# The delta-rule heads' q, k and v by seven products in the gated heads' stage, kept in DRAM, and their chains pipelined by pairs

## The chip, the cores and the metric

The kernel runs on one core of a Trainium2 chip. The metric is the device time of one execution in microseconds; the kernel before was timed in three runs. Five engines work side by side: PE (matmul, with PEld for its weight loads), DVE (vector), ACT (scalar), POOL and SP, which issues most of the DMA transfers. `order` blocks below show how instructions stand in an engine's queue, without any time; rows are line, operation, output<-inputs, and size.

## The reference

One layer of a streaming encoder on x of 1024 frames by 1024 columns, and a final norm. `h` is the normed x, and one projection of `h` gives the columns of everything in the first part:

```
q, k, v = silu(conv4(h @ [gq, gk, gv]))     # 8 delta-rule heads of 128 columns, 4 causal taps per column
S_t = a_t (I - b_t k_t k_t^T) S_{t-1} + b_t k_t v_t^T ;  o_t = S_t^T q_t      # in chunks
y_a = (rmsnorm(o) * silu(z)) @ w_branch_gdn
y_b = gated linear attention, 4 heads of 128/256 columns, @ w_branch_gla
x  += (sigmoid(gate_a) * y_a + sigmoid(gate_b) * y_b) @ w_out     # two gates of 1024 columns: 16 blocks of 128
x  += cross-attention over 256 memory rows, 4 heads
x  += relu(h @ w1)^2 @ w2
```

A delta-rule head needs per chunk the inverse of a unit lower triangular matrix made of k's products, and then a scan over the chunks that carries the state S.

## The kernel before

All data are fp32. A dense matmul splits both operands into a high and a low part and runs as three matmuls into one PSUM bank (`mm3`, lines 545, 547, 549; the splits are lines 585 on ACT and 586 on DVE or POOL). The tiles are 128 columns by 512 frames ("a half").

Two ways of projecting are in use. **Directly**, a block of 128 columns is 2 halves x 8 slices of the inner dimension x 3 = 48 matmuls of 128x512 (`g_fm`). **By seven products** (Strassen's scheme on 2x2 blocks: two column blocks, two halves; `wino_w`, `gla_dense`, `joined`), a pair of column blocks, 256 columns, is 7 products x 4 x 3 = 84, and the seven results are combined by ACT copies and DVE additions. The combinations of `h` for it lie ready in tiles `t2`, `t4`, `t6`.

The stages run one behind the other:

- `phase0`: the norm of the memory rows; K and V of the cross-attention (`K0` to `V3`, 128x256 matmuls); sums of squares, norm and splits of x; then, in the order that `ORDER` lists, the folds `Q0` to `Q3` (wq times K) and `O0` to `O3` (V times wo), kept in DRAM (`Gd`, `Ud`), and the merge gates 0 to 2. Gate 3 and the combinations of `h` follow.
- `phase_gla`: the 4 gated heads, all products by sevens; behind each head's own columns one pair of gates (`push_gate_pair`, gates 5 to 12).
- `phase_gdn`: the 8 delta-rule heads in 4 pairs. The columns k, q, v, z of each head are projected directly here (`push_conv`, `push_gdn_z`; 32 blocks); the taps read PSUM half by half (lines 1215 on ACT, 1218 on DVE, and 1221 for the columns at the seam). Per pair: decays (`gdn_decay`: `dm` loaded from the DRAM row `gcd`, its last columns copied to `gl`, lines 1233 to 1244), `gdn_keys` (transposes, norms, `kdt` at 1262, gram matrices and `NT` at 1281), `gdn_subst` (62 dependent small steps, lines 1323 and 1325), `gdn_queries`, `gdn_v`, `gdn_inverse` (1349, 1358), `gdn_scan` (8 chunks; per chunk and head the matmuls 1388, 1389, 1398, 1405, 1415 with DVE steps 1391, 1410, 1419 and ACT steps 1393, 1400 between them), and then norm, output and seven sums of the pair's result.
- `phase_merge`, `phase_out`, `phase_attn`, `phase_mlp`, which the change leaves alone.

The chains hardly fill PE, so dense products wait in a queue (`push`), and between a chain's steps `fill(n)` runs n of their matmuls; `until(name)` runs them up to the end of one product, `drain` runs all. The numbers n stand in tables (`GF`, `NFILL`, `FA` to `FI`). The kernel isn't emitted in this order, though: class `Plan` records the operations, and a list scheduler places each engine's instructions by modelled costs and by priorities that come from their matmuls' places. So an engine's final order is a result. Within an engine it is then fixed: what stands behind a waiting instruction waits too. SP's transfers are in this order as well; 32 transfers of the folds are issued by ACT.

Of the kernel before, what the change touches and what calls it, by code (L numbers as in the profile page):

```python
# [32 lines left out]
DK = 15  # L33
LA, FLU = 3, 84
# [3 lines left out]
DXB = 4  # L38
EXB, THB, GLOV, TE = 6, 1, (0, 2, 4, 6), 1
FA, FB, FC, FD, FE, FG, FH, FI = 18, 24, 30, 20, 48, 24, 3, 0  # L40
SE = ((0, 0, 0, 0, 0, 0, 0, 0), (0, 1, 0, 1, 1, 1, 0, 1), (0, 1, 0, 1, 0, 1, 0, 0))
FF = ((24, 24), (24, 24))
ORDER = ('Q0', 'Q1', 'g0', 'Q2', 'O0', 'g1', 'Q3', 'O1', 'g2', 'O2', 'O3')
XO = (('K3','V1','V3'),('V1','V3','Q1'))
# [14 lines left out]


# [4 lines left out]
GATES = (0, 1, 2, 3)  # L65
OUT = "out_0_dram"
ROUNDS, TOP, PAD, WINDOW, LOAD, HORIZON, LAND, RATE = 4, 228656, 128, 3413, 1283, 30000, 2600, 300
# [9 lines left out]
class Op:  # L77


    dma = port = False  # L80
    table = 0
# [81 lines left out]
class Plan:  # L163
    def __init__(self, tc):
        self.tc, self.marks, self.calls = tc, [], []
        self.ops, self.pools, self.tiles, self.top = [], {}, {}, {"left": [], "right": [], "psum": []}
# [118 lines left out]
    def latest(self, deps, at, end):  # L285
# [8 lines left out]
        while todo:  # L294
            i = todo.pop()
            o = ops[i]
            s = last[i] = at[i] if o.eng == "tensor" else last[i] - o.cost
# [9 lines left out]
    def forward(self, deps, prio):  # L307
# [60 lines left out]

        def take(e, now):

            q, f = now_q[e], now_q["flex"]
            if e in ("vector", "gpsimd") and f and (not q or f[0] < q[0]):
# [37 lines left out]
    def make(self):  # L410
# [4 lines left out]
        for i, ins in enumerate(self.trace()):  # L415
            while marks and marks[0].at <= i:
                self.ops.append(marks.popleft())
            if ins.engine in ENGINES and ins.opcode in OPCODES:
                self.ops.append(Op(ins, i in calls))
        self.ops += marks  # L420
# [58 lines left out]
class Layer:  # L479
# [26 lines left out]

    def psd(self):
        return self.made_in(self.ps, [P, HALF], F32, "d", self.name("pd"), 4)
# [6 lines left out]


# [54 lines left out]
    def rsqrt(self, pool, v, n):  # L571
        nc = self.nc
        y = self.til(pool, [P, 8], "rs_y", bufs=2)[:, :n]
        t = self.til(pool, [P, 8], "rs_t", bufs=2)[:, :n]
        o = self.til(pool, [P, 8], "rs_o", bufs=3)[:, :n]
# [23 lines left out]
    def wpart(self, src, shape, lo_eng=None, lp=None, before=None):  # L599

        raw = self.til(self.wp, [P] + shape, "raw", bufs=RAWS)
        hi = self.til(self.wp, [P] + shape, "wop", F32R, bufs=RING)
        lo = self.til(lp, [P] + shape, "wlo", F32R, bufs=2) if lp else \
# [84 lines left out]
    def phase0(self, xp):  # L688
        nc, a = self.nc, self.a
        with ExitStack() as ctx:  # L690
# [27 lines left out]
            def project(which, u):  # L718
                if u == 0:
                    kv[which] = self.til(sp, [P, 2, NB, MEM], "kv", F32R, bufs=2)  # L720
                dst = kv[which]
                before = [lambda i, j=j: mem_piece(2 * j + i) for j in range(2)] if len(kv) == 1 and u == 0 else [None] * 2
                w = [self.wpart(a[which][u][:, 4 * i:4 * i + 4], [4, 256], nc.vector, sp, before[i]) for i in range(2)]
# [8 lines left out]
                for j in range(2):  # L732
                    o, pt = u * 2 + j, pts[j]
                    nc.scalar.activation(dst[:, 0, o, :], pt[:, :MEM], AF.Copy)
                    nc.vector.tensor_tensor(dst[:, 1, o, :], pt[:, :MEM], dst[:, 0, o, :].bitcast(F32), SUB)

            def fold_q(h):
                kT = kv["wk"]
                w = [self.wpart(a["wqT"][h][:, :, i * HALF:(i + 1) * HALF], [2, HALF], nc.vector, sp) for i in range(2)]
                for fb in range(0, NB, 2):  # L740
                    pt = self.psd()
                    for j in range(2):
                        fs = slice((fb + j) % 4 * P, ((fb + j) % 4 + 1) * P)
                        hi, lo = w[fb // 4]
                        yield from self.mm3(pt[:, j * MEM:(j + 1) * MEM],
                                            [((hi[:, k, fs], lo[:, k, fs]),
                                              (kT[:, 0, 2 * h + k, :], kT[:, 1, 2 * h + k, :])) for k in range(2)])
                    st = self.til(sp, [P, 2, MEM], "gst", bufs=3)
                    for j in range(2):
# [1624 lines left out]
```

## Time and profile before

| | us |
|---|---|
| median of 3 runs | 2144.36 |
| lowest, highest | 2143.95, 2146.76 |
| the profiled execution, its own time | 2143.86 |
| its span in the trace | 2142.1 |
| mean granted clock of TensorE | 0.997 |
| phase 0 with gate 3, from the trace | 0 to about 158 |
| gated heads | about 158 to 553 |
| delta-rule heads | about 553 to 1092 |
| merge, output, attention, MLP | about 1092 to 2142 |

In the rows of the profile an instruction's time is its own, though matmuls overlap their neighbours, so that a row's mean times its count is more than the time that PE spends on it. In the timeline a bracket gives the engine's idle time before the row, and what released it. In the table by stretches each engine has its busy time and its count of instructions.

### The profile page before, as it was taken

To read this page: it belongs to the slowest core of one execution; us is meant where nothing else is said; L and a number is where in the kernel's file an instruction comes from. 1 tells how busy PE (TensorE), PEld (TensorE's weight loads), DVE (VectorE), ACT (ScalarE), POOL (GpSimd) and SP (SyncE) were. 2 spreads that over 40 slices of the span, in tenths; PEclk is the share of its full clock that TensorE was granted. 3 is DMA by queue.
4 is the path that set the end of the run, shared out by engine and by line. 5 is a ranking of instruction groups with operands and counts; after the bars stand their busy time and mean duration, and the time that the engine had idled before them with its cause. 6 is when DMAs were issued, how large, how long until landed. Compare 5 with 4: busy or idle time off the path is not lost.

```text
span 2142.1 us, 30977 instructions
## 1 busy us (share of the span) xinstructions
PE 2119.7 (99%) x11040; PEld 1803.8 (84%) x11040; DVE 1565.9 (73%) x2961; ACT 1173.6 (55%) x2337; POOL 169.7 (8%) x209
## 2 busy tenths in 40 slices
PE   8999999999999999999999999999999999999998
PEld 8888988988888888888888888888888888888887
DVE  7846886667685867959668899469967667567855
ACT  7445665365555646556456455565755557444433
POOL 1000000000121321313110000000000000000000
PEclk9999999999999999999999999999999999999999
DMA  7762122211311211112067662325444446778752
GB/s 257 235 230 75 61 95 81 74 65 70 123 40 50 71 44 50 59 45 74 31 221 255 229 205 89 107 81 187 131 164 148 147 149 215 225 250 288 252 176 99
DMA packets 143580, 291.75 MB, mean 136 GB/s; under 512 B 15161, under 2 KB 23737, under 8 KB 143425
## 3 DMA queue, kind: packets, MB, share of 16 engines
q1 hardware_dynamic: 134576, 281.35, 39.3%
q10 hardware_dynamic: 8848, 8.42, 1.1%
q8 instruction: 86, 1.41, 0.3%
q14 instruction: 70, 0.57, 0.1%
HBM read 208.42 MB, written 81.30 MB: 135 GB/s over the span
## 4 chain that ended last, share of the span: by engine, by line
PE 95%; DVE 2%; DMA 1%; ACT 1%; issue 0%; SPq 0%; POOL 0%; DVEq 0%; ACTq 0%
PE pd L549 22%; PE pd L545 22%; PE pd L547 22%; PE ps L547 6%; PE ps L545 6%; PE ps L549 6%; PE ps L617 2%; PE ps L1358 1%; PE ps L1278 1%; PE ps L1292 1%; PE ps L1398 1%; PE ps L1349 1%; PE ps L1415 1%; PE ps L1093 1%; PE ps L1405 1%; PE ps L1091 1%
## 5 line engine op out<-in xcount | busy, mean ns | idle before, releaser
L585 ACT ACTIVATE wop<-raw 128x512 fp32r<-128x512 f32 (+1 forms) x480 | 319.7, 671 | 402.3 <-PE pd L549 170.8
L586 DVE TENSOR_TENSOR wop<-raw,wop 128x512 fp32r<-128x512 f32 (+1 forms) x441 | 312.8, 712 | 200.7 <-ACT wop L585 195.7
L1218 DVE SCALAR_TENSOR_TENSOR acc<-pd,convw,acc 128x511 f32<-128x511 f32 x144 | 106.5, 742 | 18.3 <-ACT acc L1215 18.1
L549 PE MATMUL pd<-t,wop 128*128 128x512 f32 x236 | 94.1, 399 | 0.0
L547 PE MATMUL pd<-A1b,wop 128*128 128x512 f32 x240 | 93.6, 391 | 0.4 <-DVE A1b L586 0.4
L545 PE MATMUL pd<-A1b,wop 128*128 128x512 f32 x240 | 93.6, 391 | 0.3 <-ACT A1b L585 0.3
L547 PE MATMUL pd<-t,wop 128*128 128x512 f32 x236 | 91.9, 389 | 0.0
L545 PE MATMUL pd<-t,wop 128*128 128x512 f32 x236 | 91.7, 389 | 0.0
L549 PE MATMUL pd<-A1b,wop 128*128 128x512 f32 x228 | 88.7, 390 | 0.0
L585 ACT ACTIVATE whi<-raw 128x512 fp32r<-128x512 f32 x70 | 41.4, 625 | 55.8 <-PE pd L547 34.8
L547 PE MATMUL pd<-A1a,wop 128*128 128x512 f32 x176 | 68.6, 390 | 0.3 <-DVE A1a L586 0.3
L545 PE MATMUL pd<-A1a,wop 128*128 128x512 f32 x176 | 68.5, 389 | 0.0
L549 PE MATMUL pd<-A1a,wop 128*128 128x512 f32 x164 | 65.3, 398 | 0.0
L586 DVE TENSOR_TENSOR wlo<-raw,wop 128x1024 fp32r<-128x1024 f32 (+1 forms) x37 | 43.9, 1192 | 27.7 <-PE pd L549 13.2
L549 PE MATMUL pd<-A0b,wlo 128*128 128x512 f32 x152 | 60.9, 401 | 0.0
L549 PE MATMUL pd<-A1a,wlo 128*128 128x512 f32 x152 | 60.7, 399 | 0.0
L549 PE MATMUL pd<-A0a,wlo 128*128 128x512 f32 x152 | 60.4, 398 | 0.0
L549 PE MATMUL pd<-A1b,wlo 128*128 128x512 f32 x152 | 59.7, 393 | 0.0
L545 PE MATMUL pd<-A0a,whi 128*128 128x512 f32 x140 | 55.8, 399 | 1.0 <-ACT whi L585 1.0
L545 PE MATMUL pd<-A0b,whi 128*128 128x512 f32 x140 | 55.9, 399 | 0.0
L547 PE MATMUL pd<-A0a,whi 128*128 128x512 f32 x140 | 55.9, 399 | 0.0
L545 PE MATMUL pd<-A1a,whi 128*128 128x512 f32 x140 | 55.8, 399 | 0.0
(650 smaller groups left out, 6675.9 us busy)
## 6 DMA issues: line engine op xcount, KB each, us to landing
raw<-in_w_dram SPq DMA_DIRECT2D x120, 256.0 KB, 3.6
raw<-in_w_gdn_dram SPq DMA_DIRECT2D x64, 256.0 KB, 2.7
raw<-in_w_dram SPq DMA_DIRECT2D x32, 512.0 KB, 3.6
e<-ad SPq DMA_DIRECT2D x63, 256.0 KB, 4.5
ad<-q SPq DMA_DIRECT2D x45, 256.0 KB, 2.7
rawa<-ad SPq DMA_DIRECT2D x42, 256.0 KB, 3.7
A0b<-tgd SPq DMA_DIRECT2D x32, 256.0 KB, 5.0
ad<-acc SPq DMA_DIRECT2D x30, 256.0 KB, 2.4
```

Of the source, the lines that this page charges most:

```text
L545: nc.tensor.matmul(out, lh, rh, start=first and i == 0, stop=False, skip_group_check=True)
L547: nc.tensor.matmul(out, lh, rl, start=False, stop=False, skip_group_check=True)
L549: nc.tensor.matmul(out, ll, rh, start=False, stop=last and i == n - 1, skip_group_check=True)
L585: nc.scalar.activation(hi, raw, AF.Copy)
L586: (lo_eng or nc.gpsimd).tensor_tensor(lo, raw, hi.bitcast(F32), SUB)
L617: self.nc.tensor.transpose(pt[:, i * P:(i + 1) * P], s, self.ident)
L1091: nc.tensor.matmul(pk[:, :256], kdt[:, c, :], v[:, c, :], start=True, stop=True)
L1093: nc.tensor.matmul(po[:, :256], AT[:, c, :], v[:, c, :], start=True, stop=(c == 0))
L1218: nc.vector.scalar_tensor_tensor(x, pt[:, 0:HALF - d], tap, x, MUL, ADD)
L1278: nc.tensor.matmul(pt[:, i * P:(i + 1) * P], kc, kc, start=True, stop=True)
L1292: nc.tensor.matmul(pt[:, i * P:(i + 1) * P], k[:, 4 * g + i, :], q[:, 4 * g + i, :], start=True, stop=True)
L1349: nc.tensor.matmul(pt[:, i * 96:(i + 1) * 96], NT[:, u + i, :], PF[:, v + i, 0:96], start=True, stop=True)
```

## The change

**Projections.** The blocks q, k, v of the 8 heads, 12 pairs, and the z of heads 0 and 1 are made by seven products in the gated heads' stage (`push_extra` in place of `push_gate_pair`; `EXTRA` gives the order), and go to DRAM (`gd`). The taps run on whole 1024-wide tiles in SBUF (`taps`, one ACT copy and three DVE steps of 1023, 1022 and 1021 columns); v is turned to frames by transposes there. Gates 5 to 12 and the blocks z2 to z7 are made directly in the delta-rule stage. Over the whole program the matmuls of 128x512 in split fp32 go from 7488 to 7380; those of 128x256 (1248) and the unsplit ones keep their counts.

**Folds.** K and V, unsplit, go to DRAM (`keep`, `kvd`), and the folds run in the delta-rule stage (`fold`). `phase0` gets another order (`EV`): x's loads stand behind those of wk, and the first three gates run half by half.

**Chains.** In the delta-rule stage k, q, v, z are loaded. The substitution of pair p+1 is placed beside the scan of pair p, keys and gram matrices of p+1 ahead of the inverse of p; small operations of a pair's two heads are joined (16 wide). All chunk ends and decays come at once (`gdn_cols`): one DMA reads 64 single elements of `gcd` for each of 128 partitions. `PF` also holds the pair's output. `FILL`, `TFILL`, `PFILL`, `SFILL` say which products fill where.

**Around it.** Pools are laid out by `LAYP`, `LAYW`, `LAYQ`; the pool of `h`'s combinations is cut in three; buffers `EXB` 6 to 5, `DXB` 4 to 6; the planner runs 1 round in place of 4, `RATE` 300 to 390, can ask for matmuls earlier (`sooner`) and keep DVE back for a more urgent step (`held`). In the last gated head, a few products are placed between norm and output (`FJ`).

The core of the diff:

```diff
-    def push_gate_pair(self, sp, u, after=None):
+    def push_qv(self, sp, which, u, after=None):
...
+        def done(i, half, o, src):
+            if o is not src:
+                nc.scalar.activation(o, src, AF.Copy)
+            left[i] -= 1
+            if not left[i]:
+                y[i] = self.dxt(sp)
+                self.taps(y[i], x[i], "qkv".index(which) * GH + 2 * u + i)
+                for g in range(2):
+                    s = slice(g * HALF, (g + 1) * HALF)
+                    nc.scalar.activation(y[i][:, s], y[i][:, s], AF.Silu)
+                    if which != "v":
+                        nc.sync.dma_start(self.gd[which, u][i, :, s], y[i][:, s])
...
+        self.push(f"g{which}{u}", self.gla_dense([self.joined(dest, done)], after))
+        return turn()
...
+EXTRA = (('k', 'v', 't', 'q'), ('v', 't', 'k', 'q'), ('v', 't', 'k', 'q'), ('v', 't', 'k', 'q', 'z0'))
...
+    def taps(self, y, x, blk):
+        cw = self.convw[:, blk]
+        self.nc.scalar.activation(y, x, AF.Copy, scale=cw[:, 3:4])
+        for d in range(1, 4):
+            self.nc.vector.scalar_tensor_tensor(y[:, d:], x[:, :T - d], cw[:, 3 - d:4 - d], y[:, d:], MUL, ADD)
...
+    def gdn_cols(self, sq):
+
+        nc = self.nc
+        g = self.til(sq, [P, GH, NB], "gge", bufs=1)
+        k = self.til(sq, [P, GH, NB], "kf", bufs=1)
+        self.gge, self.kf = (t.rearrange("p h c -> p c h") for t in (g, k))
+        nc.sync.dma_start(g, self.gcd.rearrange("h (c t) -> t h c", t=P)[P - 1:P].broadcast_to([P, GH, NB]))
+        nc.vector.tensor_tensor(self.kf, self.gge, self.tm[:, :, 0], SUB)
+        nc.scalar.activation(k, k, AF.Exp)
+        nc.scalar.activation(g, g, AF.Exp)
...
+            self.gdn_cols(sq)
+            N = GH // 2
+            others(FILL[0])
+            decay(0)
+            run(near(0), PFILL[0])
+            run(self.gdn_gram(sp, heads(0)), PFILL[1])
+            PF = self.gdn_subst(sp, sq, sts[0])
+            for p in range(N):
+                others(FILL[p + 1])
...
+                if p + 1 < N:
+                    run(near(p + 1), TFILL[1])
+                run(self.gdn_queries(sq, heads(p)), TFILL[0])
+                if p + 1 < N:
+                    decay(p + 1)
+                    run(self.gdn_gram(sp, heads(p + 1)), TFILL[2])
+                run(self.sooner(self.gdn_inverse(sts[p], PF), SOON), TFILL[3])
+                if p:
+                    for h, _ in heads(p - 1):
+                        self.until(f"z{h}")
+                    run(self.gdn_out(sp, sq, p - 1, heads(p - 1)), TFILL[4])
+                if p + 1 < N:
+                    PF = self.gdn_subst(sp, sq, sts[p + 1])
+                for e, (h, st) in enumerate(heads(p)):
+                    self.gdn_v(sq, p, e, st)
...
+                for i, _ in enumerate(self.gdn_scan(sq, heads(p))):
+                    if i % 4 == 3:
+                        next(side, None)
+                    self.fill(SFILL)
...
+SFILL, PFILL, TFILL = 4, (4, 12), (4, 14, 4, 10, 12, 10)
+FILL = ((5, 6, 7, 8), ('Q0', 10, 'Q1', 'z6', 'Q2'), (9, 'O1', 'z3', 'Q3'), ('z2', 'z4', 'O0', 'z5', 11, 'O3', 'z7'), ('O2', 12, 13))
...
+EV = (('K2', 1, 'x0'), ('K3', 1, 'kk'), ('V0', 4, 'x1'), ('V1', 0, 's0'), ('V1', 8, 'n0'), ('V2', 8, 's1'), ('V3', 1, 'kv'), ('V3', 4, 'n1'))
```

The first place is the start of the delta-rule stage. SP's queue before the change, where the decays of the first two heads are loaded among weights and stores:

```order
L514 DMA raw_5375<-in_w_gdn_dram 128x512
L514 DMA raw_5379<-in_w_gdn_dram 128x512
L1622 DMA obd_69<-ex_5135 128x512
L1233 DMA dm_5189<-gcd 128x1024
L1233 DMA dm_5203<-gcd 128x1024
L514 DMA raw_5713<-in_w_gdn_dram 128x512
```

SP's queue there in the changed kernel; `gdz` is z0's place in DRAM, `gge` the new load of the chunk ends, and `raw` a gate's weights:

```order
L1016 DMA gdz_106<-dx_6020 128x512
L537 DMA k_824_6131<-gdk_103 128x1024
L537 DMA k_825_6133<-gdk_103 128x1024
L1303 DMA gge_6111<-gcd 128x64x1
L1312 DMA dm_6117<-gcd 128x1024
L1312 DMA dm_6124<-gcd 128x1024
L537 DMA k_914_6474<-gdk_107 128x1024
L537 DMA k_915_6476<-gdk_107 128x1024
L537 DMA q_6470<-gdq_104 128x1024
L537 DMA q_6472<-gdq_104 128x1024
L537 DMA raw_6566<-in_w_gate_dram 128x512
```

And DVE's queue of the changed kernel at the same place:

```order
L1304 TENSOR_TENSOR kf_6112<-gge_6111,tm_196 128x8x8
L1315 TENSOR_TENSOR dm_6117<-dm_6117,tm_196 128x1024
L1315 TENSOR_TENSOR dm_6124<-dm_6124,tm_196 128x1024
L1338 TENSOR_SCALAR vv_6220<-ssk_6135 128x16
L610 TENSOR_TENSOR rs_t_6226<-rs_y_6225 128x16
L1334 TENSOR_TENSOR kdt_827_6136<-ps_6137,kf_6112 128x512
L1334 TENSOR_TENSOR kdt_827_6136<-ps_6165,kf_6112 128x512
L1334 TENSOR_TENSOR kdt_843_6183<-ps_6184,kf_6112 128x512
L611 TENSOR_TENSOR rs_t_6226<-rs_t_6226,vv_6220 128x16
L1334 TENSOR_TENSOR kdt_843_6183<-ps_6202,kf_6112 128x512
L612 TENSOR_SCALAR rs_t_6226<-rs_t_6226 128x16
L619 TENSOR_TENSOR wlo_6565<-raw_6570,whi_6564 128x512
```

The chunk ends, which came out of `dm`, now come by a transfer of their own, ahead of `dm` on SP and at the head of this piece of DVE's queue.

The second place is the scan, on DVE. Before, in the middle of pair 0's scan, the taps of the next head's columns stand between its steps:

```order
L1410 SCALAR_TENSOR_TENSOR S_6489<-S_6417,gge_5198,ps_6487 128x128
L1410 SCALAR_TENSOR_TENSOR S_6493<-S_6421,gge_5212,ps_6491 128x128
L1419 TENSOR_TENSOR v_6086<-ps_6495,qs_6442 128x128
L1419 TENSOR_TENSOR v_6133<-ps_6500,qs_6449 128x128
L1218 SCALAR_TENSOR_TENSOR acc_6352<-pd_6359,convw_176,acc_6352 128x511
L1221 SCALAR_TENSOR_TENSOR acc_6352<-last_6353,convw_176,acc_6352 128x1
L1218 SCALAR_TENSOR_TENSOR acc_6352<-pd_6359,convw_176,acc_6352 128x510
L1391 SCALAR_TENSOR_TENSOR zh_6512<-ps_6509,gneg_180,v_6086 128x128
L1391 SCALAR_TENSOR_TENSOR zh_6519<-ps_6516,gneg_180,v_6133 128x128
```

In the changed kernel, in pair 0's scan, the steps of pair 1's substitution (`pr`, `Pm`, lines 1414 and 1416) stand there:

```order
L1504 TENSOR_TENSOR v_1031_7032<-ps_7346,qs_7300 128x128
L1504 TENSOR_TENSOR v_1032_7035<-ps_7351,qs_7307 128x128
L1414 TENSOR_TENSOR pr_6976<-X_6920,Pm_6922 128x252
L1495 SCALAR_TENSOR_TENSOR S_7340<-S_7271,gge_6111,ps_7338 128x128
L1416 TENSOR_TENSOR Pm_6922<-Pm_6922,pr_6976 128x14x18
L1495 SCALAR_TENSOR_TENSOR S_7344<-S_7275,gge_6111,ps_7342 128x128
L1414 TENSOR_TENSOR pr_6979<-X_6920,Pm_6922 128x247
L1476 SCALAR_TENSOR_TENSOR zh_7376<-ps_7373,gneg_198,v_1031_7032 128x128
L1416 TENSOR_TENSOR Pm_6922<-Pm_6922,pr_6979 128x13x19
L619 TENSOR_TENSOR wlo_7969<-raw_7974,whi_7968 128x512
L1476 SCALAR_TENSOR_TENSOR zh_7383<-ps_7380,gneg_198,v_1032_7035 128x128
```

The taps are gone from the scan, and a substitution step stands ahead of most of its operations.

598 lines of the change are left out of this document (306 added, 292 removed).

## The prediction

> **What bounds the kernel now.** I read the engines' busy time first, then the chain of waits, then the stages.
>
> ```profile
> PE 2119.7 (99%) x11040; PEld 1803.8 (84%) x11040; DVE 1565.9 (73%) x2961; ACT 1173.6 (55%) x2337; POOL 169.7 (8%) x209
> PE 95%; DVE 2%; DMA 1%; ACT 1%; issue 0%; SPq 0%; POOL 0%; DVEq 0%; ACTq 0%
> ```
>
> TensorE is busy for 99% of the span and is 95% of the chain that ended last. So the time is the number of matmuls times what one costs in a full stream, plus the few holes. What one costs is not its row's mean (390 ns): neighbours overlap. I take it from stretches in which PE did nothing but 128x512 matmuls; the table by stretches gives length, then busy time and count of PE, PEld, DVE, ACT, POOL, the granted clock, the DMA share and GB/s.
>
> ```profile
> 0.00:158.00 158.00, 146.85 (x900) 131.90 (x901) 112.30 (x187) 85.32 (x135) 10.51 (x13) 0.98 0.73 243
> 26.20:30.00 3.80, 3.80 (x20) 3.62 (x20) 2.32 (x6) 1.68 (x3) 1.93 (x1) 0.57 1.05 387
> 158.00:553.00 395.00, 394.53 (x2257) 340.80 (x2255) 278.28 (x439) 222.69 (x366) 17.83 (x21) 1.00 0.22 75
> 553.00:1092.00 539.00, 537.99 (x3216) 468.94 (x3216) 400.65 (x1016) 307.62 (x836) 114.17 (x155) 1.00 0.17 59
> 607.00:647.00 40.00, 40.00 (x207) 34.02 (x206) 38.60 (x90) 20.18 (x56) 8.90 (x16) 1.00 0.09 29
> 1700.00:1750.00 50.00, 50.00 (x222) 41.39 (x222) 32.53 (x50) 28.29 (x47) 0.00 (x0) 1.00 0.43 148
> ```
>
> In 1700 to 1750 us, 222 matmuls fill 50.00 us: **225.2 ns each**. The first 158 us are phase 0, 158 to 553 the gated heads, 553 to 1092 the delta-rule heads. PE has 11 us of holes in the first, and 0.5 and 1.0 us in the other two. In 607 to 647 us VectorE is busy for 38.6 of 40 us (pair 0's substitution) and PE still lost nothing, because dense matmuls were there to run.
>
> **The change part by part.**
>
> *Matmuls.* A pair of heads' columns costs 96 matmuls of 128x512 directly and 84 by seven products. Twelve pairs of q, k, v and one of z go from direct to seven products, four pairs of gates go back: (13 - 4) x 12 = 108 fewer, which the two programs' orders show exactly (7488 to 7380 of this shape; 128x256 and the fp32 shapes keep their counts). On a full PE that is 108 x 0.2252 = **-24.3 us**. All else is whether PE stays full.
>
> *Phase 0.* The folds, 192 matmuls of 128x256 and 96 of 128x512 (some 43 us at 0.225 us and half of it), leave for the delta-rule stage; their time is moved, not saved. What stays is the part with the holes:
>
> ```profile
> 5.50 0.79 PE L545 MATMUL pd<-mT,wop 128*128 128x256 f32 x2 [5.50 <-ACT mT L699]
> ...
> 25.31 1.05 PE L628 MATMUL ps<-ones,acc 128*128 128x1 f32 x8 [1.07 <-DVE acc L654]
> ...
> 40.99 1.02 PE L628 MATMUL ps<-ones,acc 128*128 128x1 f32 x8 [0.47 <-DVE acc L654]
> ```
>
> Two holes wait for x's sums of squares (L654). After the first of them the clock was 0.57 over 3.8 us, some 1.6 us more. The change loads x behind all of wk, and places the sums later among the products: these 3 to 5 us may go. Against that, x arrives later, its norm and splits keep their work on DVE and POOL, and the first gate's products now stand where the folds, which don't need x, gave cover. What is late next is x's split, at the first gate. I take 0; bounds -5 and +11, which is two holes like the one of 5.50 us at the start.
>
> *Gated heads' stage.* It grows by 13 pairs and loses 4. VectorE gains the products' combinations (128x512 tensor-tensor, counted 1281 to 1368) and the taps, now 72 of double width in place of 144 and their 72 end columns:
>
> ```profile
> L1218 DVE SCALAR_TENSOR_TENSOR acc<-pd,convw,acc 128x511 f32<-128x511 f32 x144 | 106.5, 742 | 18.3 <-ACT acc L1215 18.1
> L586 DVE TENSOR_TENSOR wlo<-raw,wop 128x1024 fp32r<-128x1024 f32 (+1 forms) x37 | 43.9, 1192 | 27.7 <-PE pd L549 13.2
> ```
>
> A tap on 128x1023 isn't in this trace: not under 0.742, the half-width one, nor over twice that, 1.48; I take 1.3 beside the 1.19 of the 128x1024 row, 94 us where 106.5 stood. Counting the stage's DVE rows in the new order by such durations gives an estimate of 413 us in a stage of some 545, 76%, against 278 in 395, 70%, before. Stretches at 96% (607 to 647) cost PE nothing, so 0. The 146 more SP transfers here and later (901 to 1048 in all) lie beside a DMA share of 0.22: 0.
>
> *Start of the delta-rule stage.* New is one strided load, `gge` from `gcd`: 128 partitions x 64 single elements of 4 bytes, 8192 pieces, 512 for each of 16 engines. Before, the ends came by a DVE copy out of `dm`. The load stands on SP behind the last store of z0 and the loads of k; on DVE `kf` waits for it, and behind `kf` are queued both `dm` subtractions, the `kdt` products that free four PSUM banks, and a gate's weight split. PE has 69 dense matmuls and 16 transposes between z0's last product and the first gram matmul that needs such a bank.
>
> ```profile
> 1092.73 1.09 PE L617 MATMUL ps<-ident,v 128*128 128x128 f32 x8 [0.40 <-DVE v L1443]
> ```
>
> Eight transposes take 1.09 us, so the cover is 69 x 0.2252 + 16 x 0.136 = 17.7 us. What the load itself takes must be bounded from packets of other sizes, and what follows it from the rows of before:
>
> ```profile
> q1 hardware_dynamic: 134576, 281.35, 39.3%
> ...
> oad<-sz SPq DMA_DIRECT2D x12, 256.0 KB, 2.1
> ```
>
> ```profile
> q10 hardware_dynamic: 144, 0.03, 0.4%
> ```
>
> ```profile
> 561.43 0.96 SPq L1233 DMA_DIRECT2D dm<-gcd  x2
> ```
>
> ```profile
> L1242 DVE TENSOR_TENSOR kf<-gl,tm x2: 160/166/172, 569.2 to 571.8; 128x8 f32<-128x8 f32 x2
> L1244 ACT ACTIVATE gge<-gl x2: 191/192/193, 573.2 to 573.3; 128x8 f32<-128x8 f32 x2
> ```
>
> ```profile
> L1238 DVE TENSOR_TENSOR dm<-dm,tm x8: 1217/1226/1227, 572.6 to 959.1; 128x1024 f32<-128x1024 f32 x8
> ```
>
> ```profile
> L1262 DVE TENSOR_TENSOR kdt<-ps,kf x16: 681/691/694, 580.3 to 992.2; 128x512 f32<-128x512 f32 x16
> ```
>
> No 4-byte piece is in the trace. In the first 60 us queue q10 moved 144 packets of some 200 bytes for 0.4% of 16 engines: 0.004 x 960 / 144 = 27 ns each. Packets of 2 KB on q1 over the whole span: 0.393 x 16 x 2142 / 134576 = 100 ns. So 512 pieces are 14 us by the small packets, 51 by the large ones; the lower bound is nothing seen at all, since the pieces might move as fast as their bytes. I take 14, the packets nearest in size. The load leaves some 3 us behind z0's end (the last eviction and store, and SP's issues at 0.48 each), lands at 19 with 2 us of latency (no whole transfer took less than 2.1), and then `kf` (0.2), its exponent (0.2), two `dm` (2.4) and the first `kdt` (0.7) end near 22.5: PE waits **+5 us**, bounds 0 and 42 (3 + 51 + 2 + 3.5 - 17.7). The clock stayed at 1.00 behind the 1 us holes at 553 and 1518 us; I add nothing for it.
>
> The Trainium skill, page "DMA: Bandwidth & Descriptors", section "Rules for kernel authors", says that a strided last dimension becomes one descriptor per element and should be rearranged to be contiguous; the table of its bandwidth section puts a 64-packet transfer at about 10.5 ns per packet. By that, an estimate, 8192 pieces are 86 us and the sum would be some 72 us higher; the row of q10, 27 ns on one of 16 engines (1.7 ns per packet over all 16), speaks against so much.
>
> *Delta-rule stage.* Four rounds; dense work there is 206 us (at 225 ns and half of it) where 357 were, so the chains have less beside them, some 73 us of PE per pair. And pair p+1's substitution now shares VectorE, in order, with pair p's scan.
>
> ```profile
> 1062.22 0.60 DVE L1410 SCALAR_TENSOR_TENSOR S<-S,gge,ps 128x128 f32<-128x128 f32 x2 [1.28 <-PE ps L1405]
> 1062.77 0.52 DVE L1419 TENSOR_TENSOR v<-ps,qs 128x128 f32<-128x128 f32 x2
> 1063.37 0.80 DVE L1391 SCALAR_TENSOR_TENSOR zh<-ps,gneg,v 128x128 f32<-128x128 f32 x2
> 1065.44 0.60 DVE L1410 SCALAR_TENSOR_TENSOR S<-S,gge,ps 128x128 f32<-128x128 f32 x2 [1.27 <-PE ps L1405]
> ```
>
> ```profile
> L1325 DVE TENSOR_TENSOR Pm<-Pm,pr x90: 191/332/427, 609.0 to 1032.4; 128x31 f32<-128x31 f32 x8, 128x135 f32<-128x135 f32 x8, 128x156 f32<-128x156 f32 x8, 128x240 f32<-128x240 f32 x8
> ```
>
> ```profile
> 802.98 0.74 PE L1405 MATMUL ps<-dl,kdt 128*128 128x128 f32 x4 [0.38 <-ACT dl L1400]
> ```
>
> A chunk's cycle can't be under 3.2 us (1062.22 to 1065.44), of which DVE works 1.9. In the new order PE has about 5 us of work per chunk, and DVE puts 7 or 8 substitution steps of 0.33 us into it, 1.9 + 2.6 + splits, some 5 us at most. The slack of 1.8 us per chunk takes a step of at most 0.43 ahead of each of the chunk's three hops on DVE (1.3 us). So PE should mostly stay full: bounds 0 and, with 0.43 lost twice in each of 32 chunks, 27 us. Before, taps of 0.74 us stood in the same place and PE lost 0.38 us at one of them. I take **+3**.
>
> *Rest.* Merge, output, attention and MLP keep their instructions; 0.
>
> Sum: the profiled execution took 2143.9 us (2142.1 span and 1.8 around it; 0.5 below the median of 2144.4): 2143.9 - 24.3 + 5 + 3 = 2127.6, so **2127 us**.
>
> **Rivals.**
> - *All of it hidden.* The strided load is done within the 17.7 us and the scans' steps never meet: 2143.9 - 24.3 = 2119.6, down to 2115 where x's holes go as well. For it: 539 us with 1.0 us of holes under the same kind of order. Against: dense cover shrinks by 151 us. Chance 0.22.
> - *The strided load decides (slower).* At the price of q1's packets, 100 ns, it holds back the first `kdt` until 3 + 51 + 2 + 3.5 = 59.5 us behind z0, and PE waits 42: 2143.9 - 24.3 + 42 + 3 = 2165. It turns the gain into a loss from (24.3 - 3 + 17.7 - 3 - 2 - 3.5) / 512 = 60 ns per piece. For it: a piece can cost a whole access, whatever its size. Against: the 27 ns of q10. Chance 0.12. The Trainium skill's rule on that page is of this kind; by its figure the time would be 2199.
> - *The coupled chains become the bound.* If every hop finds a substitution step ahead of it and the dense matmuls are used up, a pair loses 6 us, 2143.9 - 24.3 + 5 + 24 = 2149. For it: in-order VectorE, one `PF` for substitution, inverse and output. Against: the slack above. Chance 0.18, spread over 2132 to 2152.
> - The forecast, 2121 to 2138 with phase 0's bounds: 0.45. Other holes: 0.03.
>
> **How the numbers follow.** About 0.2%, 4.3 us, is what a measurement of this kernel can tell. Faster: 0.45 + 0.22 + 0.11 of the third rival = 0.78; same 0.07; slower 0.10 of the second and 0.05 of the third and the rest = 0.15. The range leaves out most of the second rival and the tail of the third: 2114 to 2150.
>
> **What would show it.** Right: PE still at 99%, some 108 fewer matmuls, `kf` waiting for a DMA at the stage's start and PE once for `kdt` there by about 5 us; scans 5 us per chunk. The load's landing time tells the second rival, PE idle behind DVE or ACT in scan lines the third, a hole before the first gate's products the head's bound. Wrong would be a gain with PE clearly less busy, or holes in the gated stage, where I priced 76% of VectorE at nothing.

## The result, and the profile after

| | us | ratio to before |
|---|---|---|
| before, median of 22 runs | 2145.06 (2142.95 to 2149.58) | |
| changed, median of 22 runs | 2141.95 (2137.12 to 2145.60) | 0.9983, 95% interval 0.9976 to 0.9989 |
| changed, the profiled execution | 2139.06, span 2137.4, clock 0.998 | |

The kernel is faster by some 3 us (3.1 by the medians, 3.6 by the ratio), where 18 were forecast; the two profiled executions differ by 4.8 us. The page of the changed kernel, busy time and chain:

```profile
PE 2099.2 (98%) x10932; PEld 1781.1 (83%) x10932; DVE 1598.8 (75%) x2851; ACT 1212.3 (57%) x2396; POOL 133.8 (6%) x158
PE 75%; DVE 12%; DMA 7%; issue 2%; ACT 2%; SPq 1%; POOL 1%; DVEq 0%; ACTq 0%; POOLq 0%
```

PE lost exactly the 108 matmuls (11040 to 10932) and 20.5 us of busy time, but its idle time, the span less the busy time, went from 22.4 to 38.2 us, and its part of the chain from 95% to 75%. By stages: what lies behind the delta-rule heads in the kernel before, and then the four stages of the changed kernel (phase 0, gated heads, delta-rule heads, the rest without the tail). The columns are those of the table by stretches: PE's busy time and count come first, the granted clock, the DMA share and GB/s last.

```profile
1095.00:2130.00 1035.00, 1033.82 (x4635) 857.17 (x4635) 763.39 (x1296) 554.56 (x994) 25.20 (x19) 1.00 0.55 181
```

```profile
0.00:97.00 97.00, 90.77 (x589) 83.95 (x589) 81.02 (x131) 58.34 (x103) 3.75 (x9) 1.00 0.67 245
97.00:675.00 578.00, 576.81 (x3093) 491.98 (x3092) 446.33 (x637) 342.08 (x549) 24.47 (x27) 1.00 0.26 86
675.00:1095.00 420.00, 406.74 (x2676) 360.58 (x2675) 310.64 (x782) 262.89 (x753) 82.89 (x103) 1.00 0.51 165
1095.00:2110.00 1015.00, 1005.29 (x4469) 828.10 (x4469) 741.11 (x1249) 539.89 (x971) 18.15 (x13) 1.00 0.56 180
```

Holes in phase 0 shrank from 11.2 to 6.2 us, and its clock, 0.98 over 158 us before, is 1.00, worth another 3 us. In the gated stage they went from 0.5 to 1.2, in the delta-rule stage from 1.0 to 13.3, and behind it, where no line of the kernel changed, from 1.2 to 9.7.

Six of the larger holes, from the timeline of PE in the changed kernel; the bracket has the idle time before the row and what ended it:

```profile
684.90 1.06 PE L650 MATMUL ps<-ident,k 128*128 128x128 f32 x8 [1.60 <-DMA k<-gdk]
701.07 5.47 PE L1358 MATMUL ps<-k 128*128 128x128 f32 x32 [4.67 <-DVE kdt L1334]
...
762.90 3.81 PE L1438 MATMUL ps<-PF,NT 128*128 128x96 f32 x32 [1.10 <-ACT PF L1426]
...
948.36 0.49 PE L1473 MATMUL ps<-S,k 128*128 128x128 f32 x2 [0.68 <-DVE S L1493]
...
1106.66 0.50 PE L580 MATMUL pd<-B1a,wop 128*128 128x512 f32 x1 [0.83 <-DVE B1a L619]
...
1979.58 0.47 PE L578 MATMUL pd<-B0b,wop 128*128 128x512 f32 x1 [2.07 <-DVE A0b L1797]
```

Only one, the second, is the wait that the prediction had named and sized. Behind the heads one place can be found in both programs: the start of the merge's first product (`pd<-B0a`), with 4589 matmuls from there to the end in each. First the kernel before, then the changed one:

```profile
1110.00:2142.10 1032.10, 1022.70 (x4589) 847.73 (x4587) 764.13 (x1306) 551.96 (x992) 25.88 (x20) 1.00 0.55 180
```

```profile
1092.75:2137.40 1044.65, 1027.15 (x4589) 846.49 (x4587) 763.04 (x1308) 550.45 (x995) 22.68 (x19) 1.00 0.56 179
```

The merge starts 17.2 us earlier in the changed kernel, and from there to the end it takes **12.5 us** longer, half of what the fewer matmuls save. Idle time shows only 8 us of it: the same matmuls count 4.4 us more as busy, so a matmul that waits can count as busy. The matmuls that were done show more. Three stretches of dense work, first in the kernel before and then in the changed one, which is some 17 us further in its program at the start of the first and 7 us further in the third:

```profile
1095.00:1130.00 35.00, 35.00 (x156) 28.96 (x156) 25.92 (x43) 18.96 (x35) 0.43 (x1) 1.00 0.90 313
1250.00:1275.00 25.00, 25.00 (x112) 20.72 (x111) 25.00 (x43) 14.47 (x26) 0.00 (x0) 1.00 0.66 221
1950.00:1985.00 35.00, 35.00 (x156) 28.96 (x156) 26.71 (x41) 15.74 (x27) 4.04 (x3) 1.00 0.85 279
```

```profile
1095.00:1130.00 35.00, 32.43 (x136) 24.68 (x136) 28.64 (x47) 22.39 (x39) 0.00 (x0) 1.00 0.84 274
1250.00:1275.00 25.00, 22.62 (x94) 16.89 (x93) 25.00 (x43) 11.13 (x20) 0.00 (x0) 1.00 0.39 135
1950.00:1985.00 35.00, 31.71 (x138) 25.12 (x137) 24.81 (x41) 13.62 (x24) 3.83 (x3) 1.00 0.77 248
```

Against a full stream 20, 18 and 18 matmuls are missing: 56 x 0.2252 = 12.6 us, so these three places hold about all of the loss. The sum of the profiled executions is about: -24.3 matmuls, -8 phase 0, +0.7 gated stage, +12.3 holes in the delta-rule stage, which makes -19.3 ahead of the merge where -17.2 was measured; and +12.5 behind its start. Together that is -6.8, and -4.8 was measured. The 2 us between are not assigned; waits inside the scans that don't show as idle time are a candidate.

One thing that changed there is how long ScalarE, which splits the loaded tiles, waits for them. Its idle time that ended with a load, summed from the merge's start on, is 54 us in the kernel before and 150 in the changed one.

### The profile page after: what moved, and what is told of

It reads as the page before. It is cut to its first block, busy times and chain, and to the rows that moved or that the text cites. A ratio compares the mean times of both kernels' runs of the same rounds, so it can differ in the third digit from the quotient of the medians.

```text
span 2137.4 us, 30916 instructions
## 1 busy us (share of the span) xinstructions
PE 2099.2 (98%) x10932; PEld 1781.1 (83%) x10932; DVE 1598.8 (75%) x2851; ACT 1212.3 (57%) x2396; POOL 133.8 (6%) x158
## 4 chain that ended last, share of the span: by engine, by line
PE 75%; DVE 12%; DMA 7%; issue 2%; ACT 2%; SPq 1%; POOL 1%; DVEq 0%; ACTq 0%; POOLq 0%
PE pd L578 18%; PE pd L580 18%; PE pd L582 18%; PE ps L578 4%; PE ps L582 4%; PE ps L580 4%; PE ps L650 2%; DVE wop L619 2%; PE ps L1447 1%; DMA raw<-in_w_dram 1%; DMA e<-ad 1%; PE ps L1438 1%; DMA e<-obd 1%; SPq L537 1%; PE ps L1136 1%
## 5 line engine op out<-in xcount | busy, mean ns | idle before, releaser
L619 DVE TENSOR_TENSOR wop<-raw,wop 128x512 fp32r<-128x512 f32 (+1 forms) x502 | 352.5, 706 | 189.2 <-ACT wop L618 185.3
L582 PE MATMUL pd<-t,wop 128*128 128x512 f32 x344 | 135.7, 394 | 0.0
L580 PE MATMUL pd<-t,wop 128*128 128x512 f32 x344 | 135.2, 393 | 0.2 <-DVE t L619 0.2
L578 PE MATMUL pd<-t,wop 128*128 128x512 f32 x344 | 134.1, 390 | 0.1
L578 PE MATMUL pd<-A1b,wop 128*128 128x512 f32 x276 | 107.8, 391 | 1.1 <-ACT wop L618 1.1
L580 PE MATMUL pd<-A1b,wop 128*128 128x512 f32 x276 | 107.6, 390 | 0.0
L582 PE MATMUL pd<-A1b,wop 128*128 128x512 f32 x264 | 103.0, 391 | 0.1
L1265 DVE SCALAR_TENSOR_TENSOR dx<-dx,convw,dx 128x1023 f32<-128x1023 f32 (+2 forms) x72 | 90.8, 1281 | 2.7 <-ACT dx L1263 2.5
L580 PE MATMUL pd<-A1a,wop 128*128 128x512 f32 x212 | 83.2, 393 | 0.0
L578 PE MATMUL pd<-A1a,wop 128*128 128x512 f32 x212 | 82.5, 389 | 0.0
L582 PE MATMUL pd<-A1a,wop 128*128 128x512 f32 x200 | 78.6, 393 | 0.0
L580 PEld LDWEIGHTS pd<-t,wop 128*128 128x128 f32 x344 | 64.6, 188 | 13.8 <-DVE t L619 0.5
L578 PEld LDWEIGHTS pd<-t,wop 128*128 128x128 f32 x344 | 64.6, 188 | 13.7 <-ACT t L618 0.6
L582 PEld LDWEIGHTS pd<-t,wop 128*128 128x128 f32 x344 | 64.6, 188 | 13.1
L578 PEld LDWEIGHTS pd<-A1b,wop 128*128 128x128 f32 x276 | 51.8, 188 | 12.3 <-ACT wop L618 1.9
L580 PEld LDWEIGHTS pd<-A1b,wop 128*128 128x128 f32 x276 | 51.8, 188 | 10.6
L582 PEld LDWEIGHTS pd<-A1b,wop 128*128 128x128 f32 x264 | 49.6, 188 | 10.7 <-DVE wop L619 0.5
L619 DVE TENSOR_TENSOR wlo<-raw,whi 128x512 fp32r<-128x512 f32 x58 | 39.5, 685 | 10.7 <-ACT whi L618 10.7
L931 ACT ACTIVATE dx<-pd 128x512 f32<-128x512 f32 x52 | 30.8, 593 | 29.4 <-PE pd L582 28.3
L578 PE MATMUL pd<-B0b,wop 128*128 128x512 f32 x112 | 43.8, 391 | 3.5 <-DVE A0b L1797 2.1
```

What stands on the lines that cost most here:

```text
L578: nc.tensor.matmul(out, lh, rh, start=first and i == 0, stop=False, skip_group_check=True)
L580: nc.tensor.matmul(out, lh, rl, start=False, stop=False, skip_group_check=True)
L582: nc.tensor.matmul(out, ll, rh, start=False, stop=last and i == n - 1, skip_group_check=True)
L619: (lo_eng or nc.gpsimd).tensor_tensor(lo, raw, hi.bitcast(F32), SUB)
L931: nc.scalar.activation(dest(*b), pt, AF.Copy, scale=scale)
L1265: self.nc.vector.scalar_tensor_tensor(y[:, d:], x[:, :T - d], cw[:, 3 - d:4 - d], y[:, d:], MUL, ADD)
```

## The experiments

Two constants of the planner moved with the change: rounds from 4 to 1, and `RATE`, the bytes per ns that it counts on for transfers, from 300 to 390. The prediction names no price for them. The first group tests whether they are the cause behind 1095 us (theory P), and whether the one large wait is the strided load.

**Both constants back.**

```diff
-ROUNDS, TOP, PAD, WINDOW, LOAD, HORIZON, LAND, RATE = 1, 228656, 128, 3413, 1283, 30000, 2600, 390
+ROUNDS, TOP, PAD, WINDOW, LOAD, HORIZON, LAND, RATE = 4, 228656, 128, 3413, 1283, 30000, 2600, 300
```

> The changed kernel with the planner's two constants as before: 4 rounds and a transfer rate of 300 in place of 1 and 390. Theory P: the holes of PE behind 1092 us (13.0 us over its pace in the changed kernel, 1.3 in the kernel before, though the instructions there are the same) come from these constants, which make the planner put loads nearer to their use. Then they fall under 4 us and the time is about 2132, ratio to before 0.994. Rival R: they come from elsewhere in the change (what the delta-rule stage leaves behind); then they stay at 10 or more and the time stays near 2142, ratio 0.998. The holes in the delta-rule stage (15 us) may move either way, since they are planned anew.

2129.32 us, ratio 0.9928 (0.9917 to 0.9940). The same three stretches in this kernel:

```profile
1095.00:1130.00 35.00, 31.50 (x128) 22.75 (x128) 28.05 (x46) 20.48 (x37) 0.00 (x0) 1.00 0.76 263
1250.00:1275.00 25.00, 25.00 (x112) 20.71 (x111) 25.00 (x43) 10.24 (x17) 0.00 (x0) 1.00 0.37 126
1950.00:1985.00 35.00, 35.00 (x156) 29.00 (x155) 29.58 (x49) 15.63 (x28) 2.61 (x2) 1.00 0.85 283
```

The second and third are whole again; the first lacks 28 matmuls, more than in the changed kernel. The gain was as theory P had it, its place only in part: from the merge's start to the end 1038.1 us are left, so 6.5 of the 12.5 us came back and 6.0 did not, and holes in the delta-rule stage went from 13.3 to 9.0 us as well.

**The rate alone back** (one round kept, 300).

> The changed kernel with the transfer rate alone back at 300, one round kept. If the rate is what counts within theory P, the holes behind 1092 us go as in the run with both constants back, ratio about 0.994; if the number of rounds counts, they stay above 8 us and the ratio is near 0.998. Rival R: nothing changes behind 1092 us.

2131.16 us, 0.9935 (0.9923 to 0.9946). The rate does nearly all of it; one round or four makes 2 us at most.

**The kernel before under the new constants** (1 round, 390).

> The kernel before with only the planner's constants of the changed kernel (1 round, rate 390). Theory P: holes appear behind 1092 us, some 10 us, and perhaps elsewhere; 2155 or more, ratio 1.004 to 1.008. Rival R: nothing moves behind 1092 us, ratio 0.998 to 1.002.

2158.42 us, 1.0060 (1.0047 to 1.0072): the constants alone make the old kernel 13 us slower, with 1048.6 us behind the merge's start in place of 1032.1. So the change can be compared at equal constants. With 300 and four rounds on both sides the change gives 0.9928, -15.4 us; with 390 and one round on both, 0.9983 / 1.0060 = 0.9923, -16.5 us. The forecast for the change was -24.3 + 5 + 3 = -16.3. Equal constants are not equal plans, though; what this agreement is worth is said below.

**The rate alone in the kernel before** (4 rounds, 390).

> The kernel before with the rate alone at 390, four rounds kept. If the rate is what made the kernel before slower under the new constants (1.006), the ratio is 1.004 to 1.007; if the rounds did, it is within 0.999 to 1.002.

2156.81 us, 1.0056 (1.0044 to 1.0069): the rate again, not the rounds. The longest wait of PE behind 1095 us is the same one in this run (first line) and in the changed kernel (second); the kernel before at 300 doesn't have it:

```profile
PE pd L545 <- DVE A0b L1713: 3.7, 1, 3.7
PE pd L578 <- DVE A0b L1797: 2.1, 1, 2.1
```

**The chunk ends packed.**

```diff
+        nc.sync.dma_start(self.gce.rearrange("o (h c) -> (o h) c", c=NB), gb[0:8].rearrange("p (c t) -> p c t", t=P)[:, :, P - 1])
...
-        nc.sync.dma_start(g, self.gcd.rearrange("h (c t) -> t h c", t=P)[P - 1:P].broadcast_to([P, GH, NB]))
+        nc.sync.dma_start(g.rearrange("p h c -> p (h c)"), self.gce.broadcast_to([P, GH * NB]))
```

> The changed kernel with the 64 chunk ends written packed into a DRAM row of their own when the decays are made, and read from there: 128 pieces of 256 B in place of 8192 of 4 B. The computation is the same. Theory: PE's one wait for kdt at the start of the delta-rule stage, 4.7 us in the changed kernel, is this load; it goes to under 1 us and the time falls by about 4.7 us, ratio to before about 0.996. Rival: the wait is for what stands beside it (the loads of k and dm, the norms), then 3 us or more of it stay and the ratio is near 0.998.

2134.75 us, 0.9958 (0.9944 to 0.9973), 0.25% or 5.4 us below the changed kernel. The load in the changed kernel, and SP's queue behind it:

```profile
L1303 SPq DMA_DIRECT2D gge<-gcd x1: 454/454/454, 679.7 to 679.7; - x1
L1304 DVE TENSOR_TENSOR kf<-gge,tm x1: 285/285/285, 690.3 to 690.3; 128x64 f32<-128x64 f32 x1
```

```profile
679.69 0.45 SPq L1303 DMA_DIRECT2D gge<-gcd  x1
680.19 8.81 SPq L1312 DMA_DIRECT2D dm<-gcd  x2
689.04 0.91 SPq L537 DMA_DIRECT2D k<-gdk  x2
```

What DVE did there, its idle time in brackets, and the DMA engines' busy tenths and GB/s in 40 slices of 679 to 692 us:

```profile
690.29 0.28 DVE L1304 TENSOR_TENSOR kf<-gge,tm 128x64 f32<-128x64 f32 x1 [8.47 <-DMA gge<-gcd]
693.69 1.23 DVE L1315 TENSOR_TENSOR dm<-dm,tm 128x1024 f32<-128x1024 f32 x1 [3.12 <-POOL dm L1313]
695.90 1.22 DVE L1315 TENSOR_TENSOR dm<-dm,tm 128x1024 f32<-128x1024 f32 x1 [0.98 <-POOL dm L1313]
...
700.24 0.18 DVE L610 TENSOR_TENSOR rs_t<-rs_y 128x16 f32<-128x16 f32 x1 [3.02 <-POOL rs_y L609]
700.33 1.88 DVE L1334 TENSOR_TENSOR kdt<-ps,kf 128x512 f32<-128x512 f32 x3
```

```profile
DMA  9999986759999999999999999999530869999699
GB/s 252 353 403 403 397 296 189 164 214 328 340 366 403 403 353 280 181 120 47 35 21 8 9 7 7 7 7 6 4 2 1 126 189 315 252 189 189 202 366 391
```

From 684 to 689 us the engines move mostly small packets:

```profile
DMA packets 8179, 0.20 MB, mean 40 GB/s; under 512 B 8138, under 2 KB 8138, under 8 KB 8179
```

That is the load, which has 8192 pieces; before 684 us, transfers issued ahead of it ran. So a piece costs about 0.6 ns over all engines, 9.8 on one of 16, an estimate from this line. DVE waits for the load, then twice for `dm`, and then for a power on POOL whose input stood behind `dm`; only then comes `kdt`.

And with the ends packed, the load and PE's waits at the start of the stage:

```profile
L1304 SPq DMA_DIRECT2D gge<-gce x1: 461/461/461, 678.7 to 678.7; - x1
L1305 DVE TENSOR_TENSOR kf<-gge,tm x1: 277/277/277, 684.8 to 684.8; 128x64 f32<-128x64 f32 x1
```

```profile
PE ps L1359 <- DVE kdt L1335: 1.4, 1, 1.4
```

Strided, `kf` starts 10.6 us behind the issue, packed 6.1. The wait for `kdt` falls from 4.7 to 1.4 us, where under 1 was expected. The strided load also held SP: the two issues behind it took 8.81 us, where that pair took 0.96 before, and the next loads of `k` and q and the gate's weights stood behind them. With the ends packed the pair takes 1.92.

**Packed ends and both constants back.**

> The changed kernel with the packed chunk ends and both planner constants as before (4 rounds, rate 300). If the two are separate causes, their gains add as far as the first left a wait for kdt standing (2.2 us of it in the run with the constants back): 2126 to 2128, ratio about 0.9915. Rival: with the constants back the start of the stage is limited by the loads of k and dm anyway, and nothing is added: 2129, ratio 0.993.

2125.96 us, 0.9907 (0.9893 to 0.9920), **the best of the kernels run**, 16 us below the changed one; the gains add nearly as expected. The next two runs, and three later ones, start from this kernel.

**No lead for the inverse** (`SOON` 40000 to 0, on the kernel with packed ends and constants back).

> The run with packed ends and constants back, with the lead that the inverse's work is given over other work at 0 in place of 40000 ns, so that pair p+1's substitution no longer goes first on VectorE. Theory of the coupled chains: substitution steps ahead of the scan's cost PE some 3 us in scan lines (S, zh, dl); these go, but the inverse then waits for the substitution, and the balance is worse by 3 to 10 us (ratio 0.993 to 0.997). Rival: the lead is of no use; scan holes go and the time falls by 2 to 4 us (ratio 0.990).

2134.14 us, 0.9946 (0.9934 to 0.9959), 8 us slower than with the lead, as the theory of the coupled chains had it in amount. Its place is another: the merge starts at 1086.8 us, with the lead at 1087.2, and from there to the end this run takes 5.7 us longer, in instructions that the lead doesn't touch. So the amount is chance, and the run doesn't show that the lead gains anything in the delta-rule stage.

**All of z by seven products** (same base).

```diff
-EXTRA = (('k', 'v', 't', 'q'), ('v', 't', 'k', 'q'), ('v', 't', 'k', 'q'), ('v', 't', 'k', 'q', 'z0'))
+EXTRA = (('k', 'v', 't', 'q', 'z0'), ('v', 't', 'k', 'q', 'z1'), ('v', 't', 'k', 'q', 'z2'), ('v', 't', 'k', 'q', 'z3'))
...
-FILL = ((5, 6, 7, 8), ('Q0', 10, 'Q1', 'z6', 'Q2'), (9, 'O1', 'z3', 'Q3'), ('z2', 'z4', 'O0', 'z5', 11, 'O3', 'z7'), ('O2', 12, 13))
+FILL = ((5, 6, 7, 8), ('Q0', 10, 'Q1', 'Q2'), (9, 'O1', 'Q3'), ('O0', 11, 'O3'), ('O2', 12, 13))
```

> The run with packed ends and constants back, with all four pairs of z by seven products in the gated heads' stage, not just the first: 36 matmuls of 128x512 fewer (-8.1 us at 225.2 ns), and 65 us of dense work less to run beside the chains. If PE bounds the delta-rule stage, ratio 0.988. If VectorE and the chains are near the limit there (264 us of VectorE work by the order, and PE's part falls from 367 to about 302 us), the holes grow by more than 8 us and the ratio is 0.992 or more.

2175.13 us, 1.0135 (1.0121 to 1.0149): 36 matmuls fewer and 49 us slower. The gated stage and the delta-rule stage of this kernel, and its two longest holes there:

```profile
97.00:735.00 638.00, 636.66 (x3355) 541.12 (x3354) 478.13 (x684) 366.16 (x594) 23.06 (x27) 1.00 0.27 88
735.00:1125.00 390.00, 349.58 (x2378) 309.70 (x2377) 297.18 (x760) 239.04 (x718) 89.16 (x104) 0.97 0.49 162
```

```profile
1003.31 0.80 PE L578 MATMUL pd<-whi,fold 128*128 128x512 f32 x1 [5.43 <-ACT whi L618]
...
1125.50 0.79 PE L578 MATMUL pd<-B0a,wop 128*128 128x512 f32 x1 [16.79 <-ACT wop L618]
```

40 us of idle time in one stage, 17 of them at its end, where nothing dense is left and the next stage's weights aren't there yet. VectorE is busy for 76% of the stage. The stage needs its cover; the gated stage, with VectorE at 75%, still has only 1.3 us of holes. Of the 46 us between the profiled executions, 38 lie ahead of the merge's start.

**Gates one by one in phase 0** (the two loops of `gates` exchanged, on the changed kernel).

> The changed kernel with the first three gates running both halves of one gate behind each other again, in place of all first halves and then all second ones. Theory: the head gained 11 us over the kernel before (14.5 us of excess over PE's pace to 3.7) since no product needs x's second half before it is split; then 4 us or more of waits for x's split come back at 50 to 70 us, ratio 1.000. Rival: it was the folds' leaving and x's later loads alone: under 1 us comes back, ratio 0.998.

2153.21 us, 1.0032 (1.0020 to 1.0044). The holes come where expected:

```profile
50.00:75.00 25.00, 21.42 (x131) 17.90 (x130) 23.48 (x42) 13.66 (x23) 1.32 (x1) 1.00 0.35 116
```

```profile
66.06 1.13 PE L675 MATMUL ps<-ident,rs_o 128*128 128x128 f32 x8 [1.24 <-DVE rs_o L613]
68.69 0.50 PE L578 MATMUL pd<-A1b,wop 128*128 128x512 f32 x1 [1.50 <-ACT A1b L618]
```

3.6 us in this stretch, for x's norm and its second half; the changed kernel has none there. But the whole got 11 us slower. In the profiled execution the merge starts 7.0 us later, and behind its start 6.5 us more are lost, in instructions that this edit doesn't touch. That was the first sign against a cause for each place. The last groups ask for it.

**z0 made directly too** (on the kernel with packed ends and constants back).

```diff
-EXTRA = (('k', 'v', 't', 'q'), ('v', 't', 'k', 'q'), ('v', 't', 'k', 'q'), ('v', 't', 'k', 'q', 'z0'))
+EXTRA = (('k', 'v', 't', 'q'), ('v', 't', 'k', 'q'), ('v', 't', 'k', 'q'), ('v', 't', 'k', 'q'))
...
-FILL = ((5, 6, 7, 8), ('Q0', 10, 'Q1', 'z6', 'Q2'), (9, 'O1', 'z3', 'Q3'), ('z2', 'z4', 'O0', 'z5', 11, 'O3', 'z7'), ('O2', 12, 13))
+FILL = ((5, 6, 7, 8), ('Q0', 10, 'z0', 'z1', 'Q1', 'z6', 'Q2'), (9, 'O1', 'z3', 'Q3'), ('z2', 'z4', 'O0', 'z5', 11, 'O3', 'z7'), ('O2', 12, 13))
```

> The run with packed ends and constants back, with z of heads 0 and 1 made directly in the delta-rule stage too: 12 matmuls of 128x512 more (+2.7 us), 96 of them (21.6 us) more to run beside the chains, and one pair of products less in the gated heads' stage. If what is left of the holes in the delta-rule stage (25 us of excess over PE's pace, 15 in the kernel before) is a lack of cover, they shrink by 5 us or more and the time falls to 2121 to 2124, ratio 0.989. If they are single waits that more cover at the first pair doesn't reach, the time rises by the 2.7 us, ratio 0.992.

2145.13 us, 0.9998 (0.9989 to 1.0007): 19 us slower, where +2.7 or -5 was expected. Both expectations missed.

**The rate at 250 and at 345** (same base).

> The run with packed ends and constants back, with the planner's rate at 250. Theory P as a dose: the chip's transfers ran at 269 GB/s with the DMA engines 85% busy where the merge stage waits, so a planner that counts on more is late. At 250 loads come earlier still: the holes behind 1092 us (8 us of excess) fall under 5, 2122 to 2126, ratio 0.990. Rival: 300 is enough, other loads are then in the way: no change or slower by up to 5 us, ratio 0.991 to 0.993.

> The same with the rate at 345, between the two kernels' values. Theory P as a dose: between the runs with 300 and 390, holes behind 1092 us of some 10 to 12 us, 2128 to 2131, ratio 0.9925. Rival, a step at one place: equal to the run with 300 (0.9907) or as far off as the difference that the rate made with one round (0.994 and up).

2148.28 us, 1.0012 (1.0004 to 1.0021), and 2140.37 us, 0.9973 (0.9961 to 0.9984). Both are slower than 300, by 22 and 14 us. For the time of the whole kernel theory P as a dose falls: a planner that counts on slower transfers wasn't better. Theory Q took its place: each change of the planner's inputs draws a new order for all engines, with other small holes, and the numbers in the two kernels are good draws. Four small steps test it.

**The kernel before at 310 and at 280; the changed kernel at 400 and at 380.**

> The kernel before with the planner's rate at 310 in place of 300. Theory Q: each change of the planner's inputs draws a new plan, whose small holes add up to 5 to 20 us more or less whatever the direction, and the numbers of each kernel were good draws; then ratio 1.002 to 1.008. Rival P: the rate acts by its size; a ninth of the way to 390 gives 1.000 to 1.001.

> The kernel before with the rate at 280. Theory Q: a new draw, slower like the others, ratio 1.002 to 1.008. Rival P: a lower rate makes loads earlier, ratio 0.998 to 1.000.

> The changed kernel with the rate at 400 in place of 390. Theory Q: a new draw, 4 us or more away from the changed kernel's 0.9983 or from the run at 380. Rival P: within 0.001 of 0.9983.

> The changed kernel with the rate at 380. Theory Q: a new draw, 4 us or more away from 0.9983 or from the run at 400. Rival P: within 0.001 of 0.9983.

The four ratios to the kernel before:

| | us | ratio (95%) |
|---|---|---|
| before at 310 | 2156.39 | 1.0045 (1.0028 to 1.0062) |
| before at 280 | 2150.29 | 1.0021 (1.0012 to 1.0031) |
| changed at 400 | 2151.99 | 1.0032 (1.0021 to 1.0044) |
| changed at 380 | 2148.64 | 1.0016 (1.0003 to 1.0029) |

A step of 10 or 20 in the rate costs the kernel before 10 and 5 us, and one of 10 the changed kernel 10 and 7, to either side. The changed kernel at 400, the delta-rule stage and what is behind it:

```profile
675.00:1095.00 420.00, 403.77 (x2648) 356.12 (x2648) 307.38 (x768) 257.65 (x747) 87.86 (x107) 0.99 0.50 162
1095.00:2110.00 1015.00, 1000.52 (x4416) 821.56 (x4416) 739.81 (x1247) 538.20 (x967) 17.70 (x12) 0.99 0.56 180
```

16.2 and 14.5 us of holes, with the same matmuls. That speaks for Q. Not all of the difference is holes: the profiled executions at 310 and at 400 had a granted clock of 0.995 and 0.994, where the kernel before and the changed one had 0.997 and 0.998. By clock times span, an estimate, that is 4 of 12 us and 9 of 17.

Behind the merge's start, though, P and Q both have a part. The table has the us from there to the end, the same 4589 matmuls in each, and in brackets ScalarE's idle time that ended with a load; each entry is one profiled execution:

| rate | the program before | the changed program |
|---|---|---|
| 250 | | packed ends 1049.5 (47) |
| 280 | 1032.1 (45) | |
| 300 | 1032.1 (54) | 1038.1 (99), one round 1038.5 (93), packed ends 1038.1 (86), without the lead 1043.8 (81), z0 direct 1047.5 (78) |
| 310 | 1034.9 (74) | |
| 345 | | packed ends 1043.6 (124) |
| 380 | | 1052.6 (163) |
| 390 | 1046.8 (184), one round 1048.6 (175) | 1044.6 (150), packed ends 1044.0 (159), gates by gate 1051.1 (129) |
| 400 | | 1056.8 (176) |

With a higher rate the loads come later for ScalarE in both programs, as P says, and the program before loses 15 to 17 us here at 390 and nothing at 280. Ahead of the merge it loses 6 us at 280 and 9 at 310, in the profiled executions, so most of what those two plans lose lies there. But edits that leave this part alone move it by 9 us at one rate (300), and 250 has short waits for loads and is long all the same: that is Q's scatter. Its cause stays open.

## Why the prediction was wrong

*What failed is the step "Rest. Merge, output, attention and MLP keep their instructions; 0"*, and with it that no price was set on the planner's constants, though the change names them. They keep their instructions, not their order: 12.5 us were lost there. About half of it is the rate: with 300 in place of 390, 6.5 us come back, and the program before loses 15 us in the same part when it is planned at 390. The other 6.0 us, which stay at 300, have no cause that a run here shows. As a whole the kernel before was a good draw of its planner; the same program at 280, 310 and 390 is 5 to 13 us slower. The order of the changed program lay ready; it was read at the start of the delta-rule stage and in a scan, not behind it.

*Matmuls, -24.3:* right in the count, which fell by 108; no run takes this term by itself.

*Strided load, +5:* right in place, and in size by luck: 4.67 us for `kdt`. It took 10.6 us, not 16, and its 512 pieces per engine about 5 of them, not 14, but its price came through SP's queue, which the prediction didn't name: `dm` landed late, POOL's part of `dm` and of the norm came late with it, and `kdt` started 10 us after `kf`, not some 3. The rival in which a piece costs 60 ns or more is excluded: 10.6 us / 512 is 21 ns at most. The Trainium skill, page "DMA: Bandwidth & Descriptors", section "Rules for kernel authors", advises a contiguous last dimension, and the packed row's 5.4 us agree. By the 10.5 ns per packet in the section "Bandwidth" of that page of the Trainium skill, 8192 packets one behind the other would be 86 us, an estimate. This load took 10.6 us.

*Coupled chains, +3:* too small. Of the 12.3 us of new holes in the stage, 4.7 are the strided load's and 2.7 loads of `k` (1.60 and 1.14), a wait that the prediction hadn't named; the remaining 5 are `PF`, `S`, `zh`, `whi` and the like, each under 1.2. The run with all z by sevens shows how near the limit this is: with 65 us of matmul time less in the stage, PE's idle time there is 40 us. The estimate that VectorE at 76% costs the gated stage nothing held (1.2 us; 901 to 1048 are 147 more transfers, not 146, and nothing rests on it), and the double-width taps took what was taken for them, 1.3:

```profile
L1265 DVE SCALAR_TENSOR_TENSOR dx<-dx,convw,dx 128x1023 f32<-128x1023 f32 (+2 forms) x72 | 90.8, 1281 | 2.7 <-ACT dx L1263 2.5
```

*Phase 0, 0:* too careful; it gave some 8 us by holes and clock, outside its bound of -5. Both holes before x's sums went, and so did the clock's dip behind them. That gates by halves have a part in it is shown by the run with the loops exchanged (3.6 us); what x's later loads and the folds' leaving did by themselves wasn't tried.

So the forecast was 15 us off, and that the gain at equal constants (-15.4 and -16.5 us) meets its sum of -16.3 is luck in good part. With both constants back the profiled execution gains 21.1 us ahead of the merge's start and loses 6.0 behind it, where -16.3 and 0 had been forecast: phase 0's gain, priced at nothing, stands in for the loss in the rest. In the changed kernel the -17.2 ahead of the merge meets the -16.3 in the same way, with phase 0 and the new holes of the delta-rule stage against each other. Neighbouring plans of the kernel before lie 5 to 13 us above it, those of the changed one 7 to 10 above it or 12 below; by its terms alone such a program can't be forecast closer than that.

## What to carry to other kernels

Where a scheduler decides the order, compare changes at equal scheduler settings, and try a few neighbouring settings of both kernels: a single pair of runs mixes the change with the luck of two plans. Compare the parts too, from a place that both programs have: a sum that comes out right can hide two errors. Look through the whole new order, the untouched stages too, for loads that stand nearer to their use. Work that covers a dependent chain can be worth more than the matmuls it would save elsewhere: 65 us of it moved to another stage saved 8 us of matmuls and cost 49 us in all.

## What the runs showed of the hardware

A load of 8192 single elements of 4 bytes was ready 10.6 us behind its issue, 4.5 us later than the same 64 values per partition in one run of 256 B. Where little else ran, 8138 small packets took 5 us, 9.8 ns each on one of 16 engines; such stretches move under 10 GB/s on engines that count as busy. The load also stops its issuing queue: the next two issues took 8.81 us where such a pair had taken 0.96.
